# The opening of an encoder block's projection: unit differences of the second 512 tokens taken straight from PSUM, and the later unit parts stepped one product sooner per block

## The chip, the cores and the metric

The kernel runs on one core of a Trainium2 chip. The metric is the device time of one launch in microseconds; for each kernel the median of its runs is given. Engines are named as in the profile: PE is TensorE (matmuls and transposes), PEld its weight loads, DVE is VectorE, ACT is ScalarE, POOL is GpSimd, and SP is SyncE, on whose queue nearly all DMAs are issued in order.

## The reference, cut to what matters

The kernel computes one encoder block over S = 2048 tokens of width 1024, in float32: a norm, one wide projection cut in seven parts, differential attention with four heads, retention with eight heads in both directions, an output projection, and an MLP with squared relu. The change lies in the first two lines.

```python
h = rms_norm(x, norm1_g[l])
proj = h @ w_in[l]                       # 2048 x 1024 @ 1024 x 3584
dq, dk, dv, rq, rk, rv, rg = jnp.split(proj, offsets, axis=-1)   # seven parts of 512 columns
...                                      # attention, retention, norms, gate
x = x + mix @ w_out[l]
h = rms_norm(x, norm2_g[l])
u = jax.nn.relu(h @ w_mlp1[l])
x = x + (u * u) @ w_mlp2[l]
```

## The kernel before

**The projection.** It is done in two halves of 1024 tokens (g = 0 and 1) and, in each, in seven blocks of 512 columns, in the order rq, rk, rv, rg, q, k, v. A block is 1024 features x 512 columns of weights times 1024 features x 1024 tokens. It is computed by a Winograd scheme with seven products instead of eight: both operands are cut in quarters, the weights into a11, a12, a21, a22 and the tokens' side into b11, b21 (first 512 tokens, lower and upper 512 features) and b12, b22 (second 512 tokens). The products are, in this order, a11·b11, a12·b21, s2·t2, s1·t1, s3·t3, s4·b22 and a22·t4. The second factor is called the unit of the product (`UNITS` lists them in this order), with t1 = b12 − b11, t2 = b22 − t1, t3 = b22 − b12 and t4 = t2 − b21. s1 to s4 are sums and differences of weight quarters, made on POOL by tensor_tensor (L842, L849 and L275, tiles `s`).

**High and low parts.** Every float32 operand is split in a high part (rounded by a copy to the matmul's type) and a low part (value minus high part); a product is three matmuls, high·high (L36), high·low (L37) and low·high (L38). Weight quarters are split into `wh` (ScalarE, L44) and `wl` (VectorE, L50). A unit such as t2 has the tiles `t2h` and `t2l` of 128 x 4 x 512, four slices (kp = 0 to 3) of 128 features each. In the blocks rq and rk the result comes out by features (a matmul has 512 columns), from rv on by tokens (256 columns).

**The opening.** The units of g = 0 are made before and between the products of block rq by the class `FirstUnits`, and the engines' order there is the order of the code. For each slice kp, `turn` transposes the normalised x into PSUM tiles `htp` on TensorE (L198), `bring` copies one with the gain into SBUF tiles `usrc` on ScalarE (L208), `sub` makes differences of SBUF tiles (L216), on VectorE for t1 and t2, on POOL for t3 and t4, and `split` makes the two parts of a unit on engines given by name (L44 is ScalarE's high part, L46 POOL's, L50 a low part). `rest(kp)` strings these together for a slice; `parts()` runs `rest` of slices 1 to 4 between the first products.

**The second half's units.** They are made in the blocks rk, rv, rg and q of g = 0, 256 tokens in each. `second_load` brings 256 tokens (`x2`, L873, on SP), sums their squares on ScalarE (L773) and scales them on VectorE (L878). The generator `fill_parts` then does four steps: transposes (L178) brought with the gain (L181) and b11's split; t1, t3 (L146) and the splits of b21 and b22; t2, t4 and the splits of t1 and t3; the splits of t2 and t4. Each part goes to DRAM by a store on SP (L251). A step is taken in `between(unit)`, which `winograd_block` calls after each product:

```python
if UNITS.index(unit) > 2:
    next(fill, None)
```

so the four steps stand behind the products t1, t3, b22 and t4. The `x2` of the next block is loaded on SP behind the stores of the steps before. Weight tiles `raw` and `x2` share three buffers. All of the projection's products add up in eight PSUM banks, whose results VectorE adds to partial sums `c` (L316). For q and k a result by tokens is then normalised in groups of 64 (L713) and transposed back on TensorE (L750, into `pq`, split by L58 and L59).

Of the kernel before, what the change touches and what calls it, by code (L numbers as in the profile page):

```python
# [17 lines left out]
P = 128  # L18
# [58 lines left out]
H = G // 2  # L77
# [108 lines left out]
class FirstUnits:  # L186
# [14 lines left out]
    def bring(self, kp, kh, th):  # L201
        k = kh * 4 + kp
        if (kh, th) == (0, 1):
            t = self.pool2.tile([P, H], F32, tag="hi", name="usrc")
        else:
            t = self.pool.tile([P, H], F32, tag="c", name="usrc", bufs=BUFS["c"])
# [7 lines left out]
    def sub(self, kp, n, x0, x1, o, eng):  # L214
        b = self.b[kp]
        eng.tensor_tensor(out=o, in0=b[x0], in1=b[x1], op=ALU.subtract)  # L216
        b[n] = o

    def rest(self, kp):

        nc, b = self.nc, self.b
        if kp:
            self.split(kp - 1, "t3", "act")
        if kp < 3:
            self.bring(kp + 1, 0, 1)
            self.bring(kp + 1, 1, 1)
        if kp < 4:
            t2 = self.pool2.tile([P, H], F32, tag="hi", name="t2")
            self.sub(kp, "t1", "b12", "b11", b[kp]["b11"], nc.vector)
            self.sub(kp, "t2", "b22", "t1", t2[:], nc.vector)  # L230
            self.sub(kp, "t3", "b22", "b12", b[kp]["b12"], nc.gpsimd)
        if kp:
            self.split(kp - 1, "t4", "act")
        if kp < 4:
            self.split(kp, "t2", "act")
            self.sub(kp, "t4", "t2", "b21", b[kp]["b21"], nc.gpsimd)
            self.split(kp, "t1", *(("pool",), ("act",), ("pool",), ("act",))[kp])
            self.split(kp, "b22", "act", ("dve", "pool")[kp % 2])
# [329 lines left out]
def encoder(ctx: ExitStack, tc: tile.TileContext, a: dict, out: bass.AP, dbg=None):  # L568
# [129 lines left out]
    with ExitStack() as ph:  # L698
# [133 lines left out]
        for kp in range(4):  # L832
            fu.bring(kp, 1, 0)
            fu.split(kp, "b21", "pool")
        for kp in range(3):
            for kh in range(2):
                fu.turn(kp, kh, 1)
        fu.bring(0, 0, 1)
        fu.bring(0, 1, 1)

        s1, s2 = (wp.tile([P, 4, 256], F32, tag="s", name="s") for _ in range(2))
        nc.gpsimd.tensor_tensor(out=s1[:], in0=first[1][:, 0:4], in1=first[1][:, 4:8], op=ALU.add)  # L842
        fu.rest(0)
        ahead["a12"] = split_part(first[0][:, 4:8])

        def parts():
            fu.turn(3, 0, 1)
            fu.turn(3, 1, 1)
            nc.gpsimd.tensor_tensor(out=s2[:], in0=s1[:], in1=first[0][:, 0:4], op=ALU.subtract)  # L849
            fu.rest(1)  # L850
            yield
            ahead["s2"] = split_part(s2[:])
            for kp in range(2, 5):
                fu.rest(kp)
# [785 lines left out]
```

## Time and profile before

| | before |
|---|---|
| runs | 2843.67, 2831.81 and 2831.80 us, median 2831.81 |
| profiled execution | 2833.09 us |
| its span, first to last instruction | 2831.3 us |
| mean granted TensorE clock | 0.98 |
| opening to the last block in which x2 is brought | about the first 320 us of the span |

In a row of the timeline the first number is the start in microseconds from the span's start, the second the duration; then engine, line, operation, output <- inputs, partitions x elements, and in brackets the idle time before it and what ended it. Rows of the same kind in succession are put together, with their count behind an x. A row of waits reads: engine, what waited, what it waited for, and the total, the number and the longest of these waits. In a row of a window the engines' busy times stand in the order PE, PEld, DVE, ACT, POOL, with the granted clock of TensorE, the share of the DMA engines and GB/s at its end. A row of a line's operations has the smallest, the median and the greatest duration in nanoseconds.

### The profile page before, as it was taken

Reading aid. Unit: us, or ns where it says so; the run is one execution under the profiler, and the core shown is the slowest. Engines: PE = TensorE matmul, PEld = TensorE weight load, DVE = VectorE, ACT = ScalarE, POOL = GpSimd, SP = SyncE. Lnnn points to the kernel's source line nnn. Section 1 sums busy time; section 2 is a strip of 40 time slices with the busy share of each in tenths; the row PEclk is TensorE's granted clock in tenths of the full one; section 3 lists DMA queues with packets and bytes.
Section 4 is the critical chain, followed back from the end, with each engine's and each line's share of the span. In section 5 each row is a group of like instructions: output and inputs, shape, how many; then the busy total and the mean of one; then the engine's idle time right before and its main releaser. Section 6 shows DMA issues by size and latency. Waiting matters only on the chain.

```text
span 2831.3 us, 41049 instructions
## 1 busy us (share of the span) xinstructions
PE 2716.9 (96%) x15488; PEld 2332.9 (82%) x15488; DVE 1914.4 (68%) x2877; ACT 1297.6 (46%) x1842; POOL 1350.9 (48%) x778
## 2 busy tenths in 40 slices
PE   5998999998879999999898999999999999999999
PEld 4898889998768888888787788888888888888887
DVE  7878864587779999999898467665555534435442
ACT  5343432344457777777533255544445432222221
POOL 5326222613348787778544366765655104323320
PEclk8999999999899999999999999999999999999999
DMA  3555693249623131421368668767444858755471
GB/s 127 165 178 157 203 331 120 92 139 268 167 68 98 38 98 40 102 91 60 127 216 275 255 226 270 233 251 264 144 160 168 296 174 289 279 194 178 156 245 45
DMA packets 361029, 494.50 MB, mean 175 GB/s; under 512 B 23168, under 2 KB 257152, under 8 KB 352640
## 3 DMA queue, kind: packets, MB, share of 16 engines
q1 hardware_dynamic: 338608, 466.71, 50.4%
q10 hardware_dynamic: 21648, 20.98, 2.2%
q0 software_dynamic: 576, 4.19, 0.4%
q8 instruction: 122, 2.00, 0.3%
q14 instruction: 75, 0.61, 0.1%
HBM read 315.64 MB, written 176.16 MB: 174 GB/s over the span
## 4 chain that ended last, share of the span: by engine, by line
PE 75%; DVE 7%; DMA 4%; ACT 1%; issue 1%; POOL 1%; SPq 0%; ACTq 0%; DVEq 0%; POOLq 0%
PE ps L38 10%; PE ps L36 10%; PE ps L37 10%; PE p L38 7%; PE p L36 7%; PE p L37 7%; PE pa L1214 4%; PE sc L1020 4%; PE sc L1021 4%; PE po L36 2%; PE po L38 2%; PE po L37 2%; DVE kvs L493 1%; PE mm L38 1%; PE mm L37 1%
## 5 line engine op out<-in xcount | busy, mean ns | idle before, releaser
L37 PE MATMUL p<-wl,ah 128*128 128x512 f32 x896 | 348.6, 389 | 0.0
L36 PE MATMUL p<-wh,ah 128*128 128x512 f32 x896 | 348.5, 389 | 0.0
L275 POOL TENSOR_TENSOR s<-raw 128x1024 f32<-128x1024 f32 x58 | 147.6, 2545 | 402.5 <-DMA raw<-in_w_in 143.0
L50 DVE TENSOR_TENSOR wl<-s,wh 128x1024 fp32r<-128x1024 f32 x120 | 191.6, 1599 | 183.9 <-ACT wh L44 183.7
L316 DVE TENSOR_TENSOR c<-ps,c 128x512 f32<-128x512 f32 x360 | 238.4, 684 | 113.7 <-PE ps L38 111.6
L1053 POOL TENSOR_TENSOR p<-p 128x1024 f32<-128x1024 f32 x127 | 303.4, 2413 | 0.1
L44 ACT ACTIVATE ah<-ra 128x1024 fp32r<-128x1024 f32 x112 | 112.6, 1052 | 412.4 <-PE p L37 410.8
L1037 ACT ACTIVATE p<-p,nm 128x2048 f32<-128x2048 f32 x128 | 256.9, 2007 | 36.4 <-DVE nm L1025 35.1
L50 DVE TENSOR_TENSOR ah<-ra,ah 128x1024 fp32r<-128x1024 f32 x76 | 102.7, 1387 | 219.2 <-ACT ah L44 219.2
L1463 POOL TENSOR_TENSOR c<-c 128x512 f32<-128x512 f32 x128 | 196.4, 1560 | 111.3 <-ACT c L1466 101.8
L1524 POOL TENSOR_TENSOR t<-br 128x1024 f32<-128x1024 f32 x32 | 76.8, 2400 | 336.4 <-DMA br<-in_w_mlp 168.4
L38 PE MATMUL p<-wh,ah 128*128 128x512 f32 x608 | 236.6, 389 | 0.0
L44 ACT ACTIVATE wh<-s 128x1024 fp32r<-128x1024 f32 x120 | 126.4, 1056 | 200.0 <-PE ps L37 103.0
L1052 POOL TENSOR_SCALAR p<-p,ratio 128x1024 f32<-128x1024 f32 x127 | 141.9, 1131 | 143.3 <-DVE ratio L1047 111.2
L1020 PE MATMUL sc<-ka,qa 128*128 128x512 f32 x512 | 207.6, 406 | 2.6 <-DVE nm L1025 2.6
L1021 PE MATMUL sc<-ka,qb 128*128 128x512 f32 x512 | 202.9, 396 | 0.0
L37 PEld LDWEIGHTS p<-wl,ah 128*128 128x128 f32 x896 | 168.2, 188 | 34.9
L36 PEld LDWEIGHTS p<-wh,ah 128*128 128x128 f32 x896 | 168.2, 188 | 34.8
L55 ACT ACTIVATE aTh<-pa 128x512 fp32r<-128x512 f32 x256 | 151.2, 591 | 82.6 <-PE pa L1214 81.4
L1025 DVE CUSTOM_DVE_ANT_0 p<-sc,bias,nm 128x1024 f32<-128x1024 f32 (+1 forms) x136 | 167.7, 1233 | 22.6 <-PE sc L1021 20.8
L1214 PEld LDWEIGHTS pa<-ident,p 128*128 128x128 f32 x1024 | 121.1, 142 | 64.6 <-issue 30.7
L56 DVE TENSOR_TENSOR aTl<-pa,aTh 128x512 fp32r<-128x512 f32 x256 | 170.2, 686 | 4.4 <-DMA vh<-vhd 3.6
(377 smaller groups left out, 8164.9 us busy)
## 6 DMA issues: line engine op xcount, KB each, us to landing
br<-in_w_mlp SPq DMA_DIRECT2D x88, 512.0 KB, 5.3
raw<-in_w_mlp SPq DMA_DIRECT2D x32, 1024.0 KB, 5.9
raw<-in_w_in SPq DMA_DIRECT2D x28, 1024.0 KB, 5.9
xt<-in_x SPq DMA_DIRECT2D x20, 512.0 KB, 5.3
q<-rqd SPq DMA_DIRECT2D x16, 512.0 KB, 10.2
qa<-qhd SPq DMA_DIRECT2D x64, 128.0 KB, 2.9
qb<-qld SPq DMA_DIRECT2D x64, 128.0 KB, 3.0
ua11d<-c SPq DMA_DIRECT2D x32, 256.0 KB, 3.4
```

The costliest lines, as they stand in the source:

```text
L36: nc.tensor.matmul(out, ah, bh, start=first, stop=False)
L37: nc.tensor.matmul(out, ah, bl, start=False, stop=False)
L38: nc.tensor.matmul(out, al, bh, start=False, stop=last)
L44: nc.scalar.activation(hi, src, AF.Copy)
L50: e.tensor_tensor(out=lo, in0=src, in1=hi.bitcast(F32), op=ALU.subtract)
L316: nc.vector.tensor_tensor(out=o[:], in0=x0[:], in1=x1[:], op=op)
L1020: nc.tensor.matmul(sc[:, o : o + 512], qa[:, c, ql], r, start=True, stop=False)
L1021: nc.tensor.matmul(sc[:, o : o + 512], qb[:, c, ql], r, start=False, stop=True)
L1037: nc.scalar.activation(p[:], p[:], AF.Exp, bias=nm[:, n : n + 1], scale=-1.0, accum_out=l[:])
L1053: e.tensor_tensor(out=p0, in0=p0, in1=p1, op=ALU.add)
L1214: nc.tensor.transpose(pa[:, j], p0[:, kt * P : (kt + 1) * P], ident[:])
L1463: nc.gpsimd.tensor_tensor(out=u[n][:], in0=u[x0][:], in1=u[x1][:], op=op)
```

## The change

It has three parts. First, in the opening, the second 512 tokens' values no longer pass through SBUF for the differences: a new `times` computes gain · PSUM − x by one scalar_tensor_tensor on VectorE, for t1, t2, t3 and for the low part of b22 (L214 of the new kernel); `first` copies b12 and makes the high part of b22 straight from PSUM on ScalarE (L230, L232). The high parts of t1 to t4 are all ScalarE's (`high`, L225), their low parts VectorE's (`low`, L222); t4's subtraction stays on POOL (L243). Two of the four high parts of b21 go to ScalarE. Second, the order in the opening: a12's split moves ahead of the first slice's unit work, and the transposes of slices 2 and 3 move from ahead of and within b11's product to behind b21's. Third, the fill steps start behind t1 in block rk as before, behind t2 in rv, behind b21 in rg, and behind b11 in q.

```diff
--- before.py
+++ after.py
@@ -200,10 +200,7 @@
 
     def bring(self, kp, kh, th):
         k = kh * 4 + kp
-        if (kh, th) == (0, 1):
-            t = self.pool2.tile([P, H], F32, tag="hi", name="usrc")
-        else:
-            t = self.pool.tile([P, H], F32, tag="c", name="usrc", bufs=BUFS["c"])
+        t = self.pool.tile([P, H], F32, tag="c", name="usrc", bufs=BUFS["c"])
         ps = self.turned.pop((kp, kh, th))
         self.nc.scalar.activation(t[:], ps[:], AF.Copy, scale=self.gain[:, k : k + 1])
         self.b[kp][f"b{kh + 1}{th + 1}"] = t[:]
@@ -211,31 +208,52 @@
     def split(self, kp, n, hi, lo="dve"):
         split_sbuf(self.nc, *(t[:, kp] for t in self.tb[n]), self.b[kp][n], hi, lo)
 
-    def sub(self, kp, n, x0, x1, o, eng):
-        b = self.b[kp]
-        eng.tensor_tensor(out=o, in0=b[x0], in1=b[x1], op=ALU.subtract)
-        b[n] = o
+    def times(self, kp, kh, n, x, o):
+
+        k = kh * 4 + kp
+        self.nc.vector.scalar_tensor_tensor(
+            out=o, in0=self.turned[kp, kh, 1][:], scalar=self.gain[:, k : k + 1], in1=x, op0=ALU.mult, op1=ALU.subtract
+        )
+        if n is not None:
+            self.b[kp][n] = o
+
+    def low(self, kp, n):
+        th, tl = (t[:, kp] for t in self.tb[n])
+        self.nc.vector.tensor_tensor(out=tl, in0=self.b[kp][n], in1=th.bitcast(F32), op=ALU.subtract)
+
+    def high(self, kp, n):
+        self.nc.scalar.activation(self.tb[n][0][:, kp], self.b[kp][n], AF.Copy)
+
+    def first(self, kp):
+        nc, k = self.nc, 4 + kp
+        b12 = self.pool2.tile([P, H], F32, tag="hi", name="usrc")
+        nc.scalar.activation(b12[:], self.turned[kp, 0, 1][:], AF.Copy, scale=self.gain[:, kp : kp + 1])
+        self.b[kp]["b12"] = b12[:]
+        nc.scalar.activation(self.tb["b22"][0][:, kp], self.turned[kp, 1, 1][:], AF.Copy, scale=self.gain[:, k : k + 1])
 
     def rest(self, kp):
 
         nc, b = self.nc, self.b
+        if kp < 4:
+            b12 = b[kp]["b12"]
+            hi, lo = (t[:, kp] for t in self.tb["b22"])
+            self.times(kp, 0, "t1", b[kp]["b11"], b[kp]["b11"])
+            t2 = self.pool2.tile([P, H], F32, tag="hi", name="t2")
+            self.times(kp, 1, "t2", b[kp]["t1"], t2[:])
+            nc.gpsimd.tensor_tensor(out=b[kp]["b21"], in0=b[kp]["t2"], in1=b[kp]["b21"], op=ALU.subtract)
+            b[kp]["t4"] = b[kp]["b21"]
+            self.times(kp, 1, "t3", b12, b12)
+            self.times(kp, 1, None, hi.bitcast(F32), lo)
+            if (kp + 1, 0, 1) in self.turned:
+                self.first(kp + 1)
+            for n in ("t2", "t1", "t3"):
+                self.high(kp, n)
         if kp:
-            self.split(kp - 1, "t3", "act")
-        if kp < 3:
-            self.bring(kp + 1, 0, 1)
-            self.bring(kp + 1, 1, 1)
+            self.high(kp - 1, "t4")
+            self.low(kp - 1, "t4")
         if kp < 4:
-            t2 = self.pool2.tile([P, H], F32, tag="hi", name="t2")
-            self.sub(kp, "t1", "b12", "b11", b[kp]["b11"], nc.vector)
-            self.sub(kp, "t2", "b22", "t1", t2[:], nc.vector)
-            self.sub(kp, "t3", "b22", "b12", b[kp]["b12"], nc.gpsimd)
-        if kp:
-            self.split(kp - 1, "t4", "act")
-        if kp < 4:
-            self.split(kp, "t2", "act")
-            self.sub(kp, "t4", "t2", "b21", b[kp]["b21"], nc.gpsimd)
-            self.split(kp, "t1", *(("pool",), ("act",), ("pool",), ("act",))[kp])
-            self.split(kp, "b22", "act", ("dve", "pool")[kp % 2])
+            for n in ("t2", "t1", "t3"):
+                self.low(kp, n)
 
 
 def into_dram(nc, pool, tag, saved, j, tb=None):
@@ -831,25 +849,29 @@
         ahead = {"a11": split_part(first[0][:, 0:4])}
         for kp in range(4):
             fu.bring(kp, 1, 0)
-            fu.split(kp, "b21", "pool")
-        for kp in range(3):
+        for kp in range(4):
+            fu.split(kp, "b21", ("pool", "act")[kp % 2])
+        for kp in range(2):
             for kh in range(2):
                 fu.turn(kp, kh, 1)
-        fu.bring(0, 0, 1)
-        fu.bring(0, 1, 1)
 
         s1, s2 = (wp.tile([P, 4, 256], F32, tag="s", name="s") for _ in range(2))
         nc.gpsimd.tensor_tensor(out=s1[:], in0=first[1][:, 0:4], in1=first[1][:, 4:8], op=ALU.add)
+        fu.first(0)
+        ahead["a12"] = split_part(first[0][:, 4:8])
         fu.rest(0)
-        ahead["a12"] = split_part(first[0][:, 4:8])
 
         def parts():
-            fu.turn(3, 0, 1)
-            fu.turn(3, 1, 1)
             nc.gpsimd.tensor_tensor(out=s2[:], in0=s1[:], in1=first[0][:, 0:4], op=ALU.subtract)
             fu.rest(1)
             yield
+            yield
             ahead["s2"] = split_part(s2[:])
+            yield
+            for kp in range(2, 4):
+                for kh in range(2):
+                    fu.turn(kp, kh, 1)
+            fu.first(2)
             for kp in range(2, 5):
                 fu.rest(kp)
             opening.close()
@@ -925,7 +947,7 @@
                 def between(unit):
                     if g and what == "v":
                         lead_in(unit)
-                    if UNITS.index(unit) > 2:
+                    if UNITS.index(unit) > 3 - bi:
                         next(fill, None)
 
                 winograd_block(nc, wp, pp, raws, tb, what not in ("rq", "rk"), consumer(what, g), later, between,
```

On VectorE the opening's row from the first slice on was this before (`wl_392` is a12's low part, `t2_380` and `t2_425` are t2 of slices 0 and 1):

```order
28 L216 TENSOR_TENSOR usrc_287<-usrc_369,usrc_287 128x512
29 L216 TENSOR_TENSOR t2_380<-usrc_371,usrc_287 128x512
30 L50 TENSOR_TENSOR t2l_212<-t2_380,t2h_211 128x512
31 L50 TENSOR_TENSOR t1l_214<-usrc_287,t1h_213 128x512
32 L50 TENSOR_TENSOR b22l_218<-usrc_371,b22h_217 128x512
33 L50 TENSOR_TENSOR wl_392<-raw_203,wh_391 128x1024
34 L50 TENSOR_TENSOR t3l_216<-usrc_369,t3h_215 128x512
35 L216 TENSOR_TENSOR usrc_291<-usrc_376,usrc_291 128x512
36 L216 TENSOR_TENSOR t2_425<-usrc_378,usrc_291 128x512
```

and is this after:

```order
28 L50 TENSOR_TENSOR wl_366<-raw_203,wh_365 128x1024
29 L214 SCALAR_TENSOR_TENSOR usrc_287<-htp_339,g1_153,usrc_287 128x512
30 L214 SCALAR_TENSOR_TENSOR t2_370<-htp_344,g1_153,usrc_287 128x512
31 L214 SCALAR_TENSOR_TENSOR usrc_362<-htp_344,g1_153,usrc_362 128x512
32 L214 SCALAR_TENSOR_TENSOR b22l_218<-htp_344,g1_153,b22h_217 128x512
33 L222 TENSOR_TENSOR t2l_212<-t2_370,t2h_211 128x512
34 L222 TENSOR_TENSOR t1l_214<-usrc_287,t1h_213 128x512
35 L222 TENSOR_TENSOR t3l_216<-usrc_362,t3h_215 128x512
36 L214 SCALAR_TENSOR_TENSOR usrc_291<-htp_349,g1_153,usrc_291 128x512
37 L214 SCALAR_TENSOR_TENSOR t2_399<-htp_354,g1_153,usrc_291 128x512
```

The low part of a12 has moved from behind the first slice's lows to ahead of everything of that slice, and four operations of a slice read a PSUM tile `htp`. On POOL the row from b21 on was, before (`usrc <- usrc` is t3, `usrc <- t_380,usrc` is t4):

```order
L46 TENSOR_SCALAR b21h<-usrc 128x512 x4
L842 TENSOR_TENSOR s<-raw 128x1024
L216 TENSOR_TENSOR usrc<-usrc 128x512
L216 TENSOR_TENSOR usrc<-t_380,usrc 128x512
L46 TENSOR_SCALAR t1h<-usrc 128x512
L849 TENSOR_TENSOR s<-s,raw 128x1024
L275 TENSOR_TENSOR s<-raw,s 128x1024
L216 TENSOR_TENSOR usrc<-usrc 128x512
L216 TENSOR_TENSOR usrc<-t_425,usrc 128x512
```

and is after:

```order
L46 TENSOR_SCALAR b21h<-usrc 128x512 x2
L859 TENSOR_TENSOR s<-raw 128x1024
L243 TENSOR_TENSOR usrc<-t_370,usrc 128x512
L865 TENSOR_TENSOR s<-s,raw 128x1024
L293 TENSOR_TENSOR s<-raw,s 128x1024
L243 TENSOR_TENSOR usrc<-t_399,usrc 128x512
```

Two highs of b21, t3 and t1's highs have left POOL's row. On TensorE, in block rv, the 16 transposes of x2 stood between t1's and t3's products:

```order
L36 MATMUL ps<-wh,t1h 128x256
L37 MATMUL ps<-wl,t1h 128x256
L38 MATMUL ps<-wh,t1l 128x256
L178 MATMUL htp<-ident,x_1109 128x128 x16
L36 MATMUL ps<-wh,t3h 128x256
L37 MATMUL ps<-wl,t3h 128x256
L38 MATMUL ps<-wh,t3l 128x256
```

and stand between t2's and t1's now:

```order
L36 MATMUL ps<-wh,t2h 128x256
L37 MATMUL ps<-wl,t2h 128x256
L38 MATMUL ps<-wh,t2l 128x256
L178 MATMUL htp<-ident,x_1101 128x128 x16
L36 MATMUL ps<-wh,t1h 128x256
L37 MATMUL ps<-wl,t1h 128x256
L38 MATMUL ps<-wh,t1l 128x256
```

They have moved up by one product there; in the blocks rg and q they move up by two and by three.

## The prediction

> **What bounds the kernel now.** I read the page's totals first, then the waits of TensorE by stage, then the rows that end those waits.
>
> ```profile
> span 2831.3 us, 41049 instructions
> PE 2716.9 (96%) x15488; PEld 2332.9 (82%) x15488; DVE 1914.4 (68%) x2877; ACT 1297.6 (46%) x1842; POOL 1350.9 (48%) x778
> ```
>
> TensorE is busy for 96% of the span, so only its gaps, some 114 us, and slices at a lower clock can be won. The change touches the first 320 us, so I take TensorE's waits of 12 to 140 us (the opening), and of 111.8 to 330 us (the blocks in which the second 1024 tokens are filled).
>
> ```profile
> PE ps L38 <- DVE wl L50: 9.0, 3, 6.8
> PE ps L37 <- DVE t1l L50: 1.6, 1, 1.6
> PE ps L37 <- DVE t2l L50: 1.5, 1, 1.5
> PE ps L36 <- ACT t2h L44: 1.3, 1, 1.3
> ```
>
> ```profile
> PE pq L750 <- DVE c L713: 13.1, 2, 8.6
> PE ps L37 <- DVE wl L50: 5.7, 3, 2.4
> PE htp L178 <- DVE x L878: 2.3, 1, 2.3
> ```
>
> Nearly all of them end on VectorE. The opening ends for VectorE with the low part of s4's weights, for which the b22 product waits:
>
> ```profile
> 44.53 0.79 PE L38 MATMUL ps<-b21h,wl 128*128 128x512 f32 x1 [6.76 <-DVE wl L50]
> 80.32 0.49 PE L38 MATMUL ps<-b22h,wl 128*128 128x512 f32 x1
> 79.05 1.21 DVE L50 TENSOR_TENSOR wl<-s,wh 128x1024 fp32r<-128x1024 f32 x1
> ```
>
> Why VectorE is late there is seen in two pairs of rows, one pair with SBUF sources, one with PSUM sources:
>
> ```profile
> 37.70 2.33 POOL L849 TENSOR_TENSOR s<-s,raw 128x1024 f32<-128x1024 f32 x1
> 37.77 2.82 DVE L50 TENSOR_TENSOR t1l<-usrc,t1h 128x512 fp32r<-128x512 f32 x1 [1.76 <-POOL t1h L46]
> 43.26 1.21 DVE L50 TENSOR_TENSOR wl<-raw,wh 128x1024 fp32r<-128x1024 f32 x1
> 44.40 0.68 DVE L50 TENSOR_TENSOR t3l<-usrc,t3h 128x512 fp32r<-128x512 f32 x1
> 80.18 1.28 DVE L316 TENSOR_TENSOR c<-ps,c 128x512 f32<-128x512 f32 x2
> 80.40 2.40 POOL L275 TENSOR_TENSOR s<-raw,s 128x1024 f32<-128x1024 f32 x1 [4.82 <-DVE wl L50]
> ```
>
> A subtraction of two SBUF tiles takes 0.68 us alone (t3l) and 2.82 us when a POOL sum of 2.33 us runs (t1l ends 0.56 us after that sum). The two adds from PSUM, however, took 0.64 us each though POOL's sum covered most of them. I read it so: VectorE with two SBUF operands and POOL's tensor_tensor take turns; VectorE with one operand in PSUM does not wait.
>
> **The opening, part by part.** Removed: ScalarE's copy of b22 in each of the four slices (its high comes straight from PSUM), and on POOL four t3 subtractions, two b22 lows, two t1 highs. Added on VectorE: the four t3 and the two b22 lows that were POOL's; t1, t2, t3 and b22's low, 16 operations, now read PSUM. Added on ScalarE: two t1 highs and two b21 highs, less four copies, so it does no more than before, and at 46% of the span it has room. The price of the new form is not in the trace with this source; the nearest are these:
>
> ```profile
> 309.78 0.73 DVE L59 SCALAR_TENSOR_TENSOR lo<-pq,qg,hi 128x512 fp32r<-128x512 f32 x1
> 308.74 2.38 POOL L275 TENSOR_TENSOR s<-raw,s 128x1024 f32<-128x1024 f32 x1 [3.08 <-DVE wl L50]
> L316 DVE TENSOR_TENSOR c<-ps,c x12: 674/676/681, 76.7 to 86.8; 128x512 f32<-128x512 f32 x12
> 57.28 1.29 POOL L216 TENSOR_TENSOR usrc<-usrc 128x512 f32<-128x512 f32 x1 [1.23 <-DVE usrc L216]
> 27.43 5.51 DVE L50 TENSOR_TENSOR b21l<-usrc,b21h 128x512 fp32r<-128x512 f32 x4
> ```
>
> L59 is the same instruction (scalar times PSUM, minus SBUF): 0.73 us, inside a POOL sum of 308.74 to 311.12 and not held by it. Bounds: 0.68 us (a plain add from PSUM) and 2.8 us (if POOL holds it after all); I take L59's 0.73, or 0.67 from start to start, since successive rows overlap by some 0.07.
>
> With 0.67 per PSUM operation, 0.60 per free SBUF one, 1.15 per weight low, 2.35 per POOL sum and 1.25 per POOL subtraction, VectorE's new row runs as follows. The b21 lows end at 32.9 as before with a12's low now directly behind them: POOL does two highs instead of four, so it reaches its first sum about 1.2 us earlier, which pays for the 1.15. That low came at 43.26 to 44.47 before, and TensorE stood 6.76 us for it. Slice 0: four PSUM operations to 35.7, then t2, t1, t3 lows alternate with POOL's s2 and s4 sums (2 x 2.35) and its t4: 42.2. Slice 1: PSUM operations to 44.9, the late t4 low of slice 0 (ScalarE makes its high last) 46.4, three lows 48.2. Weight lows of s2 and s1, and slice 2's t1 from PSUM, one held by a POOL sum: 52.9. Slice 2's other three from PSUM, s3's low, four lows: 58.4. Slice 3's four: 61.1. Its predecessor's t4 low held by two sums for the next block's weights: 63.0. POOL's t4 64.2, remaining lows 66.6, four adds 69.0, s4's low 70.2. Before, that low ended at 80.26. The lead is **−10.1 us**. The lower bound of the gain is found by letting POOL hold the PSUM operations too: POOL's sums in that stretch would cost another 7.7 us, and 2.4 are left; the upper is 11 with 0.68 per operation less its overlap. TensorE can follow: its waits above (9.0 + 1.6 + 1.5 + 1.3 = 13.4) are more than the lead. The sixteen transposes of slices 2 and 3 move behind b21's product, but are the same in number; what was hidden on their account stays inside VectorE's row.
>
> [...]
>
> [...]
>
> **The fill steps.** Each of the next four blocks turns 256 tokens of the second half in four steps. All four blocks began them after the product t1; now the second, third and fourth begin one, two and three products sooner. No instruction is added. With its step move VectorE's and POOL's subtractions (L146), ScalarE's highs and the stores on SP; the stores pass the loads of the next block's weights, which are behind buffers in use, and POOL, 48% busy, takes its two subtractions a fill between weight sums. I put both at nothing so long as x2 is the last to come; it has its own term below. Old stalls first:
>
> ```profile
> 153.07 1.91 PE L178 MATMUL htp<-ident,x 128*128 128x128 f32 x16
> 154.83 0.36 PE L36 MATMUL ps<-wh,t3h 128*128 128x256 f32 x1
> 307.09 0.56 PE L36 MATMUL ps<-wh,t1h 128*128 128x256 f32 x1
> 147.31 0.28 PE L36 MATMUL ps<-wh,t1h 128*128 128x256 f32 x1
> 180.60:184.30 3.70, 3.70 (x19) 3.70 (x20) 3.39 (x5) 0.00 (x0) 0.16 (x1) 0.54 0.56 156
> 249.10:252.90 3.80, 3.35 (x17) 2.98 (x17) 3.66 (x6) 0.73 (x2) 0.00 (x0) 0.55 0.12 39
> 285.57 0.45 PE L750 MATMUL pq<-ident,c 128*128 128x128 f32 x1 [8.57 <-DVE c L713]
> ```
>
> A token-major product takes 5.75 us (147.31 to 153.07 holds one), sixteen transposes 1.76. From 153.07 to 307.09 there are 20 products, three sets of 16 transposes (5.3) and q's own transposes (L750), which I put at 3.5: 123.8 us of work in 154.0. So 30.2 us are lost, of them 21.1 as the waits above and the rest, 9.1, mostly as half clock (0.54 and 0.55 in two windows, behind waits of 2.3 us). The longest wait, 8.57, comes from VectorE's lateness in block q, where a fill step is done between 253 and 285.5:
>
> ```profile
> L50 DVE TENSOR_TENSOR hi<-x,hi 128x512 fp32r<-128x512 f32 x5 | 4.5, 893 | 0.0
> L181 DVE TENSOR_TENSOR x<-htp,g 128x512 f32<-128x512 f32 x4 | 2.6, 688 | 0.0
> L146 DVE TENSOR_TENSOR x<-x 128x512 f32<-128x512 f32 x2 | 1.8, 898 | 0.0
> ```
>
> These 8.9 us of VectorE's work move three products, 17 us, ahead, and the norm of q (L713) meets a free engine. Likewise the weight lows at a block's end (5.7) no longer meet the last fill step. I let 8.4 stand: what the two L750 waits leave beyond the 8.57 (13.1 − 8.6, say 5 with new ones), and two half-clock spells of 1.7. Gain **−21.8**, bounds 8.6 (that one wait alone) and 30.2.
>
> Now what comes in its place. TensorE asks for x2 sooner; x2 comes through SP's queue behind the last store of the fill before, is squared by ScalarE and scaled by VectorE.
>
> ```profile
> 137.67 0.59 SPq L873 DMA_DIRECT2D x<-in_x  x1
> 150.21 1.42 DVE L878 TENSOR_SCALAR x<-x,ss 128x1024 f32<-128x1024 f32 x2
> 183.73 0.95 SPq L873 DMA_DIRECT2D x<-in_x  x1
> 194.77 1.42 DVE L878 TENSOR_SCALAR x<-x,ss 128x1024 f32<-128x1024 f32 x2
> 249.16 0.64 PE L178 MATMUL htp<-ident,x 128*128 128x128 f32 x2 [2.32 <-DVE x L878]
> ```
>
> In rv the transposes now stand where t1 began, 147.31, and the first half of x2 is scaled at 150.9 (half of the 1.42 row): a wait of 3.6. Both shift with the opening's lead, since rk's steps keep their places. In rg and q the round from one set of transposes to the next has 36.3 us (six products and 1.76). It needs 1.76, three products (17.25), about 6 for the last split and its store (the last step no longer sits at the block's end), 1.5 on the queue, 11.1 from x2's issue to its scaling (183.73 to 194.77), and 0.7: 38.3. So 2.0 each. Half clock costs 1.7 behind the first wait (the 180.60 window: 3.7 x 0.46). Behind waits of 2.0, a little shorter than those for which a row shows it, it costs between 0 and 1.7 each; I take the middle, 1.7 for both. Price **+11.0**, from 3.6 (the two rounds fit) to 28.3 (the first rival).
>
> [...]
>
> **Sum.** −10.1 − 21.8 + 11.0 = −20.9 against the profiled execution's 2833.1: 2812.2. That execution lies 1.3 above the median of the runs, so 2811.
>
> **The rivals.** First, x2 takes all back: if the rounds stay as long as before (153.07 to 195.5 is 42.4, 199.25 to 249.16 is 49.9), the waits are 3.6 + 6.1 + 13.6 and 5 of half clock, 28.3 in all; −3.6, or 2828. For it: SP's queue is in order and x2 stands behind the stores. Against: those two rounds contained the very stalls that go. Second, PSUM operations are held by POOL too: lead 2.4, 2819. Against it stand L59 and the 80.18 row. Third, slower: the x2 wait feeds itself. Each round as long as the longest, 49.9, because the scaling (L878) stands in VectorE's row behind weight lows that themselves wait for POOL's sums of weights, whose load is behind x2 on SP: 3 x 13.6 + 5 = 45.8, net +13.9, 2846. It decides once the three waits with their clock pass 31.9. Only one round of three showed this length. A fourth, that the DVE row is no bound for TensorE in the opening, is refuted by the waits quoted.
>
> **How the numbers follow.** Forecast 0.67, first rival 0.18, second 0.08, third 0.07. A change below 0.5% (14.2 us, 2817.7 to 2846) can hardly be told from none. The forecast's own range is 2799 (all 30.2 gained, waits near 6) to 2820, with about a tenth of its chance above 2817.7; rivals one and two lie within 0.5%. So faster 0.60, same 0.33, slower 0.07. The range is 2799 to 2829: it takes in rivals one and two and leaves out the third and the ends.
>
> **What would show it.** The b21 product without the 6.76 wait; SCALAR_TENSOR_TENSOR from `htp` at 0.73 to 0.75 while POOL runs; the b22 product at s4's low ten us sooner; no long L750 wait in q; new waits of the L178 transposes on x in rv near 3.6 and in rg and q near 2. Waits there of 6 and more would show the first rival or the third; PSUM rows of 2 us and more the second.

## The result and the profile after

The changed kernel takes 2816.5 us (median of five runs, 2814.8 to 2820.8) against 2834.9 for the kernel before in the same comparison (2831.8 to 2843.7): the ratio is 0.994, interval 0.9929 to 0.9951, or 18.4 us less. The forecast was 2811, and faster. The profiled execution of the changed kernel took 2819.9, 3.4 above its median, with a span of 2818.2.

The page's totals and TensorE's waits, first in the opening (12 to 140 us), then in the blocks in which the second half is filled (100 to 330 us), after the change (lines of the new kernel: L198 and L178 are the same transposes, L900 was L878, L768 was L750, L731 was L713). The waits for the normalised x ahead of the first products stand in both kernels, 17.7 us before and 16.7 after, and are left out:

```profile
span 2818.2 us, 41052 instructions
PE 2716.7 (96%) x15488; PEld 2332.3 (83%) x15488; DVE 1906.4 (68%) x2883; ACT 1298.4 (46%) x1844; POOL 1329.9 (47%) x768
```

```profile
PE htp L198 <- DVE usrc L214: 2.8, 1, 2.8
PE ps L36 <- DVE usrc L214: 2.3, 1, 2.3
PE ps L36 <- ACT wh L44: 1.6, 1, 1.6
PE ps L37 <- DVE t1l L222: 1.5, 1, 1.5
PE htp L198 <- DVE b22l L214: 1.1, 1, 1.1
PE ps L36 <- DVE b22l L214: 0.6, 1, 0.6
```

```profile
PE htp L178 <- DVE x L900: 11.0, 3, 6.9
PE pq L768 <- DVE rst L71: 1.2, 1, 1.2
PE pq L768 <- DVE c L731: 0.9, 1, 0.9
PE ps L36 <- DVE lo L59: 0.4, 1, 0.4
```

The 6.8 us for a12's low are gone, but new waits of 9.9 us stand in the opening, four of the six on operations that read PSUM (L214). In the fill, 21.1 us of waits have become 13.5, of which 11.0 are for x2. Three marks divide the span, the first scores of the attention (L1020, now L1042), the last of that line, and the first matmul of the MLP (L36 into `p`). Of before, then of the changed kernel:

```profile
L1020 PE MATMUL sc<-ka,qa x512: 388/396/795, 794.9 to 1355.2; 128*128 128x512 f32 x171
...
L36 PE MATMUL p<-wh,ah x896: 388/389/390, 2217.9 to 2826.5; 128*128 128x512 f32 x180
```

```profile
L1042 PE MATMUL sc<-ka,qa x512: 389/396/792, 778.4 to 1338.8; 128*128 128x512 f32 x171
...
L36 PE MATMUL p<-wh,ah x896: 389/389/389, 2204.8 to 2813.4; 128*128 128x512 f32 x180
```

With the first transposes of x2 in rk (111.8 before, 107.0 after) the 13.1 us of the two profiled spans split so: 4.8 in the opening, 11.7 from there to the attention, nothing in the attention, 3.3 given back between its end and the MLP (862.7 us before, 866.0 in this execution). This last loss looks like this execution's own and not the change's: in the eight other kernels of the table whose POOL rows stand there in the same order (before, opening only, SBUF source, sums behind, a12 first, POOL relieved, gain on VectorE, same late order) the stretch takes 862.2 to 863.4 us. The experiments are read by the same marks:

| run | opening, lead | to the attention | attention's end to MLP | median against before in the same comparison |
|---|---|---|---|---|
| before | 0 | 683.1 | 862.7 | |
| changed | 4.8 | 671.4 | 866.0 | −18.4 |
| opening only | 4.9 | 682.9 | 863.2 | −6.5 |
| steps only | −1.0 | 670.1 | 872.2 | −3.4 |
| SBUF source | 5.4 | 671.7 | 863.4 | −19.6 |
| sums behind | 7.9 | 676.3 | 862.2 | −19.7 |
| q later | 3.8 | 670.6 | 862.5 | −15.2 |
| a12 first | 0.3 | 683.9 | 863.0 | +0.5 |
| POOL relieved | 4.4 | 680.0 | 863.3 | −5.0 |
| one gate multiplication (one run) | 8.3 | 663.2 | 861.9 | −29.3 |
| relief and steps | 4.6 | 670.4 | 872.8 | −7.0 |
| gain on VectorE | 7.6 | 668.1 | 862.7 | −22.6 |
| gate on VectorE | 7.7 | 667.0 | 869.1 | −17.4 |
| same late order | 3.4 | 671.2 | 862.7 | −13.4 |

The stages are of one profiled execution each; the last column is of the timed runs. The changed kernel, opening only and q later have the same opening, and its lead is 4.8, 4.9 and 3.8. In q later VectorE's row there is only 0.1 us later, but behind the wait of 2.3 us at t3's product TensorE's granted clock was 0.67 from 64.1 to 71.6 us, where the changed kernel's was 0.81. So leads that differ by 1 us are not told apart.

### The profile page after: what moved, and what is told of

It is laid out like the page before. It is cut to its first block, busy times and chain, and to the rows that moved or that the text cites. A ratio compares the mean times of both kernels' runs of the same rounds, so it can differ in the third digit from the quotient of the medians.

```text
span 2818.2 us, 41052 instructions
## 1 busy us (share of the span) xinstructions
PE 2716.7 (96%) x15488; PEld 2332.3 (83%) x15488; DVE 1906.4 (68%) x2883; ACT 1298.4 (46%) x1844; POOL 1329.9 (47%) x768
## 4 chain that ended last, share of the span: by engine, by line
PE 79%; DVE 7%; DMA 2%; issue 1%; ACT 1%; POOL 1%; SPq 0%; ACTq 0%; DVEq 0%; POOLq 0%
PE ps L38 11%; PE ps L36 11%; PE ps L37 11%; PE p L38 7%; PE p L36 7%; PE p L37 7%; PE pa L1236 4%; PE sc L1042 4%; PE sc L1043 4%; PE po L36 2%; PE po L38 2%; PE po L37 2%; DVE kvs L511 1%; PE mm L38 1%; PE mm L37 1%
## 5 line engine op out<-in xcount | busy, mean ns | idle before, releaser
L36 PE MATMUL p<-wh,ah 128*128 128x512 f32 x896 | 348.4, 389 | 0.0
L1042 PE MATMUL sc<-ka,qa 128*128 128x512 f32 x512 | 207.5, 405 | 3.2 <-ACT yt L575 2.7
L36 PEld LDWEIGHTS p<-wh,ah 128*128 128x128 f32 x896 | 168.2, 188 | 34.9
L1047 DVE CUSTOM_DVE_ANT_0 p<-sc,bias,nm 128x1024 f32<-128x1024 f32 (+1 forms) x136 | 167.7, 1233 | 22.6 <-PE sc L1043 21.0
## 6 DMA issues: line engine op xcount, KB each, us to landing
q<-rqd SPq DMA_DIRECT2D x16, 512.0 KB, 10.1
```

The lines of the kernel that those rows point to most:

```text
L36: nc.tensor.matmul(out, ah, bh, start=first, stop=False)
L1042: nc.tensor.matmul(sc[:, o : o + 512], qa[:, c, ql], r, start=True, stop=False)
```

## The experiments

My theory after the result was that both parts work as forecast, and that the opening is 5 us short because two POOL sums for the next block's weights run in the middle of it. The rival was that reading PSUM keeps the banks and makes TensorE the bound.

**The two parts alone.** First the changed kernel with the old fill steps:

```diff
-                    if UNITS.index(unit) > 3 - bi:
+                    if UNITS.index(unit) > 2:
```

> The changed opening with the old fill steps (behind t1 in all four blocks). If the two parts are worth what the trace of the changed kernel shows, block rk's first transposes of x2 come at 107.0 us of the span as there (111.8 before), a lead of 4.8, the stalls from 153 to 307 us stay, and the time is 4.8 us under before, about 2830. The rival: the lead lets the middle run differently, x2 and the weights come relatively sooner and part of the old stalls goes too; then 8 to 13 us under before.

2828.3 against 2834.7, ratio 0.9978 (0.9970 to 0.9987). By stage it is the theory: a lead of 4.9, 682.9 us to the attention as before. Then the reverse, the kernel before with the new steps:

```diff
-                    if UNITS.index(unit) > 2:
+                    if UNITS.index(unit) > 3 - bi:
```

> The kernel before with only the earlier fill steps. The two traces give 195.3 us from rk's transposes to the start of k's t1 product before and 185.5 after: if that stretch's gain is the steps' own, the time is 9.8 us under before, about 2825. The rival: the gain needs the opening's lead (x2 of rv comes later against the products), then waits for x2 of about 11 take the gain back and the time is within 3 us of before.

2831.3 against 2834.7, ratio 0.9984 (0.9975 to 0.9992): only 3.4 less, which looks like the rival, but isn't. From rk's transposes to the attention it takes 13.0 us less than before, 10.8 of them up to k's t1 product; x2's waits did not take it back. It lost 9.5 far behind, between the attention and the MLP. TensorE's waits there, of before (1355.2 to 2217.9) and of this run (1344.3 to 2216.5):

```profile
PE mt L1186 <- POOL mx L1177: 2.8, 4, 0.9
...
PE mt L1186 <- POOL mx L1176: 2.0, 2, 1.3
```

```profile
PE mt L1186 <- POOL mx L1176: 11.9, 6, 3.5
...
PE mt L1186 <- POOL mx L1177: 1.2, 3, 0.6
```

`mt` are the transposes of the attention's and retention's mixed output ahead of the output projection. No line of that code differs. The rows do: the built program of this run has POOL's multiplications of `mx` (L1176, L1177) behind a low part of the next units, where they stood ahead of it (`+` is this run's place):

```order
 L1379 TENSOR_SCALAR early<-xt_15393,rs_15777 128x1024
-L1176 TENSOR_TENSOR mx<-mx,dog 128x512
-L1177 TENSOR_TENSOR mx<-mx,gates 128x512
 L50 TENSOR_TENSOR hl_15845<-quads,hl_15844 128x512
+L1176 TENSOR_TENSOR mx<-mx,dog 128x512
+L1177 TENSOR_TENSOR mx<-mx,gates 128x512
```

So the order of a stage that the scheduler arranges changed with an edit more than 1000 us ahead of it. In the changed kernel it did not. The last experiment tests this.

**Where the operands come from.** In the changed kernel b12 and b22 are copied to SBUF by ScalarE, and VectorE's differences read the copies (ScalarE's added copy of b22 is not shown here):

```diff
-        self.nc.vector.scalar_tensor_tensor(
-            out=o, in0=self.turned[kp, kh, 1][:], scalar=self.gain[:, k : k + 1], in1=x, op0=ALU.mult, op1=ALU.subtract
-        )
+        self.nc.vector.tensor_tensor(out=o, in0=self.b[kp][f"c{kh + 1}2"], in1=x, op=ALU.subtract)
```

> The changed kernel, but b12 and b22 are copied to SBUF by ScalarE first, and t1, t2, t3 and b22's low on VectorE are plain subtractions of SBUF tiles in the same order. If reading PSUM is what lets VectorE run beside POOL, the operations that now run during POOL's four t4 subtractions (1.3 us each) must take turns with them: 5.2 us more in VectorE's row, less 16 x 0.06 for the shorter form, so 4 us over the changed kernel, with nearly all of its lead in the opening gone. The rival: the PSUM tiles now come free by ScalarE, the transposes behind b21 no longer wait (2.8 and 1.2 us in the changed kernel), and the form costs less, so the time is the same or up to 3 us less.

2815.1 against 2834.7, ratio 0.9928 (0.9916 to 0.9941): not told apart from the changed kernel's 0.994. Both readings were right in their part, and they cancel. b22's low of slice 0, first in the changed kernel, then from SBUF beside POOL's t4:

```profile
35.34 0.74 DVE L214 SCALAR_TENSOR_TENSOR b22l<-htp,g,b22h 128x512 fp32r<-128x512 f32 x1
```

```profile
34.58 1.62 POOL L243 TENSOR_TENSOR usrc<-t,usrc 128x512 f32<-128x512 f32 x1 [4.97 <-DVE t L213]
...
34.95 1.79 DVE L213 TENSOR_TENSOR b22l<-usrc,b22h 128x512 fp32r<-128x512 f32 x1
```

From SBUF it is held by POOL, about 1.0 us in each of four slices, and VectorE's last low ends at 71.5 instead of 70.0. But in the changed kernel t3's product on TensorE waits for VectorE to read a bank (L214 makes t1 of slice 3 there, which t3's product doesn't need, and in the run from SBUF this wait is gone, so I put it down to the bank), and then VectorE waits 1.6 us for that product's result:

```profile
64.02 0.77 PE L36 MATMUL ps<-t3h,wh 128*128 128x512 f32 x1 [2.33 <-DVE usrc L214]
...
71.64 0.69 DVE L334 TENSOR_TENSOR c<-ps,c 128x512 f32<-128x512 f32 x1 [1.63 <-PE ps L38]
```

The result is the same to within what is measured. (The transposes' waits for banks, 2.8 and 1.2 us, cost nothing of their own: t2's product starts at 48.0, and at 48.4 in the run from SBUF, where it waits for s2's high part instead.)

**The next block's sums.** In the changed kernel these two sums are put behind slice 3's t4 on POOL; no row of VectorE or TensorE moves:

```diff
-        nc.gpsimd.tensor_tensor(out=t[:], in0=wa[x0], in1=wa[x1], op=op)
+        with behind(n):   # for s1, s2 of block rk: tc.issue_after(fu.last.ins)
+            nc.gpsimd.tensor_tensor(out=t[:], in0=wa[x0], in1=wa[x1], op=op)
```

> The changed kernel with POOL's two sums for the next block's weights (2.6 and 2.7 us at 57.3 and 60.0 us) put behind the t4 subtraction of slice 3; nothing else moves on VectorE or TensorE. If these sums are why the opening's lead was 5 us short, slice 2's t1 and t3 lows take 0.7 us instead of 2.9 each, VectorE's row is 4.4 us earlier from there, TensorE's wait of 2.3 at t3's product goes, and the time is 3 to 4.5 us under the changed kernel. The rival: TensorE's own row, with its transposes that waited for PSUM banks, is the bound by then (VectorE stood 1.6 us waiting for it at 71.6), and the time is less than 1 us under, or over if the sums then come late for block rk.

2815.0 against 2834.7, ratio 0.9926 (0.9913 to 0.9940). The lead at rk is 7.9 instead of 4.8 (7.6 and 7.7 in two later runs with the sums behind), so the sums do cost the opening some 3 us, as the theory had it. VectorE and POOL of the changed kernel, then with the sums behind:

```profile
57.32 2.56 POOL L293 TENSOR_TENSOR s<-raw 128x1024 f32<-128x1024 f32 x1 [1.96 <-DMA raw<-in_w_in]
57.57 2.86 DVE L222 TENSOR_TENSOR t1l<-usrc,t1h 128x512 fp32r<-128x512 f32 x1
59.96 2.70 POOL L293 TENSOR_TENSOR s<-s,raw 128x1024 f32<-128x1024 f32 x1
60.36 2.85 DVE L222 TENSOR_TENSOR t3l<-usrc,t3h 128x512 fp32r<-128x512 f32 x1
```

```profile
57.28 0.68 DVE L222 TENSOR_TENSOR t1l<-usrc,t1h 128x512 fp32r<-128x512 f32 x1
57.88 0.68 DVE L222 TENSOR_TENSOR t3l<-usrc,t3h 128x512 fp32r<-128x512 f32 x1
```

The time, however, did not fall by 3 to 4.5. k's t1 product still starts 3.0 us earlier than in the changed kernel (289.5 and 292.5), though q's x2 waits 9.1 instead of 6.9 us. Then 4.8 us are lost on the way to the attention. TensorE's wait for ScalarE in the retention there, in the changed kernel and with the sums behind:

```profile
PE rt L573 <- ACT yT L565: 4.6, 1, 4.6
```

```profile
PE rt L574 <- ACT yT L566: 10.3, 2, 6.6
```

That is 5.7 us in a stage whose rows are the same in both; why ScalarE came later there I have not traced.

**Order alone and load alone.** The kernel before with a12's split ahead of the first slice:

```diff
+        ahead["a12"] = split_part(first[0][:, 4:8])
         fu.rest(0)
-        ahead["a12"] = split_part(first[0][:, 4:8])
```

> The kernel before with nothing changed but a12's split put ahead of the first slice's unit work. If the order is what gives the opening's lead, b21's wait of 6.8 us for that low part goes and rk's first transposes come 4 to 5 us earlier, like the changed opening alone. The rival: VectorE and POOL have the same work to do in turns, the unit lows come later by what the weight low takes, and the lead is at most 1.5 us (the low takes 1.2).

2834.3 against 2833.8, ratio 1.0003 (0.9994 to 1.0011), a lead of 0.3. The rival was right: the wait moved one product on and grew from 6.8 to 9.7.

```profile
48.91 0.79 PE L36 MATMUL ps<-t2h,wh 128*128 128x512 f32 x1 [9.73 <-ACT wh L44]
```

Then the kernel before in its order and from SBUF, with POOL's work taken away as in the change, at three places of the code:

```diff
-            fu.split(kp, "b21", "pool")
+            fu.split(kp, "b21", ("pool", "act")[kp % 2])
-            self.sub(kp, "t3", "b22", "b12", b[kp]["b12"], nc.gpsimd)
+            self.sub(kp, "t3", "b22", "b12", b[kp]["b12"], nc.vector)
-            self.split(kp, "t1", *(("pool",), ("act",), ("pool",), ("act",))[kp])
-            self.split(kp, "b22", "act", ("dve", "pool")[kp % 2])
+            self.split(kp, "t1", "act")
+            self.split(kp, "b22", "act")
```

> The kernel before in its old order and from SBUF copies, but POOL relieved as in the change: t3 and all b22 lows on VectorE, all t1 highs and two b21 highs on ScalarE. POOL loses some 4 x 1.25 + 2 x 1.25 + 4 x 0.6 = 9.9 us, VectorE gains 6 x 0.6 = 3.6; if taking turns is the bound, the sum of both rows is 6 us shorter and the lead at rk's transposes is 4 us or more. The rival: only the order brings the lead, and here it is under 1.5 us, or negative, since VectorE's own row is longer.

2828.8 against 2833.8, ratio 0.9985 (0.9976 to 0.9994), a lead of 4.4. To within what leads can tell, that is the whole of the opening's 4.8: POOL's relief is enough for it, without the PSUM source and without the new order. VectorE's own row did gain by the other two, since its last low part ends at 76.7 us before, at 73.2 with relief alone, at 71.5 in the run from SBUF (relief and order) and at 70.0 in the changed kernel. TensorE did not follow, and little of that reached block rk.

**q's x2.** Its transposes waited 6.9 us where I had put 2. One try gives it a product more:

```diff
-                    if UNITS.index(unit) > 3 - bi:
+                    if UNITS.index(unit) >= (0, 3, 2, 1, 1, 0, 0)[bi]:
```

> The changed kernel with block q's steps one product later (behind b21, as in rg; rk and rv as changed). If x2 of q is ready at 228.7 us whatever TensorE asks, its transposes stand then after the b21 product (end at 227.4) and wait 1.3 instead of 6.9 and 0.6, and the half clock behind them goes: k's t1 product 5 to 6 us earlier, and the time 4 to 6 us less. The rival: the fill's work on VectorE moves against q's own norms, whose waits (8.6 before, 1.2 and 0.9 in the changed kernel) come back by as much, and the time is within 2 us of the changed kernel.

2818.6 against 2833.8, ratio 0.9947 (0.9934 to 0.9959): no better than the changed kernel. x2's wait fell to 1.7 and 1.1, but q's norms wait again, as the rival had it:

```profile
261.60 0.45 PE L768 MATMUL pq<-ident,c 128*128 128x128 f32 x1 [5.80 <-DVE c L731]
```

The other try leaves out the gate's second multiplication on POOL (the output lacks the retention's norm gain):

```diff
-                    nc.gpsimd.tensor_tensor(
-                        out=t3, in0=t3, in1=gng[:, c0 : c0 + 256].unsqueeze(1).to_broadcast([P, 2, 256]), op=ALU.mult
-                    )
```

> The changed kernel without the second POOL multiplication of the gate (by the retention's group norm gain) in block rg, of both halves, so the output lacks that factor. If POOL's multiplications hold VectorE's small operations and the scaling of q's x2 (from 221.4 to 230.2 us, where 6 to 7 us pass for 2.4 us of work), the wait of q's transposes falls from 6.9 to 4 us or less. The rival: x2 of q is late by its load and by ScalarE's queue (its squares end at 219.4), and the wait stays between 6 and 7.5.

One run of 2804.5. q's x2 waited 2.4 us and then 1.1. In the changed kernel, two rows of x2's chain beside the gate's multiplications:

```profile
224.47 2.31 POOL L750 TENSOR_TENSOR c<-c,gng 128x512 f32<-128x512 f32 x1
...
225.59 1.22 DVE L73 SCALAR_TENSOR_TENSOR ss<-rst,ss 128x2 f32<-128x2 f32 x1
226.84 3.39 DVE L900 TENSOR_SCALAR x<-x,ss 128x1024 f32<-128x1024 f32 x2
```

Here an operation on 128 x 2 elements takes 1.22 us, which took 0.16 at 145.23 us, where POOL was idle, and the scaling 3.39 instead of 1.42. So the rows show the theory's mechanism, POOL's gate holding x2's chain, but it is not the whole of the shorter wait. From its first small operation to the end of the scaling the chain took 10.6 us in the changed kernel (219.65 to 230.23) and 8.6 without the second multiplication. The longest hold in it, 2.26 us for another operation on 128 x 2 elements, lay beside a weight sum of POOL (222.18 to 224.51), and it stayed. Of the 4.4 us by which the wait fell, some 2.0 are the chain's. The rest came because x2's load was issued 6.7 us sooner (203.2 instead of 209.9) while TensorE asked only 4.2 sooner; why it was, I have not traced. By accident this run showed more. In its opening the first sum for the next block started at 57.68 instead of 57.32, 0.02 after slice 2's t1 low had started:

```profile
57.68 2.91 POOL L293 TENSOR_TENSOR s<-raw 128x1024 f32<-128x1024 f32 x1 [2.23 <-DMA raw<-in_w_in]
...
57.66 0.68 DVE L222 TENSOR_TENSOR t1l<-usrc,t1h 128x512 fp32r<-128x512 f32 x1
58.27 2.87 DVE L222 TENSOR_TENSOR t3l<-usrc,t3h 128x512 fp32r<-128x512 f32 x1
```

One turn fell the other way, and rk's transposes came at 103.5 instead of 107.0. Of these 3.5 us the turn gave 2.1, the time by which VectorE's last low ends earlier (67.9 instead of 70.0). For the rest TensorE's granted clock was 1.00 instead of 0.81 from 64.1 to 71.6 us, behind a wait of 2.0 instead of 2.3.

**A version meant to do more.** The changed kernel with the sums behind, and with that second multiplication on VectorE instead:

```diff
-                    nc.gpsimd.tensor_tensor(
+                    nc.vector.tensor_tensor(
                         out=t3, in0=t3, in1=gng[:, c0 : c0 + 256].unsqueeze(1).to_broadcast([P, 2, 256]), op=ALU.mult
```

> The changed kernel with the next block's two sums behind slice 3 (as in the run of that edit alone) and the gate's second multiplication in rg moved from POOL to VectorE. On POOL it takes 1.3 to 1.7 us in which VectorE's SBUF work waits, on VectorE 0.7: eight of them in the first half, 5 us less of turns, most of it between 196 and 235 us. Then the wait of q's transposes (9.1 with the sums behind) falls to 5 or less and the time is 4 to 5 us under that run, near 2810. The rival: VectorE's row gets longer just ahead of x2's scaling, the wait stays above 7, and the time is within 1.5 us of that run.

2811.7 against 2834.4, ratio 0.9926 (0.9912 to 0.9939), 3.3 below the run with the sums behind by medians, whose ratio is the same; so the two are not told apart. The reason I gave is refuted: q's x2 waits 10.4 us, not 5, since the multiplications now stand in VectorE's own row ahead of the scaling. The gain to the attention (668.1 instead of 676.3) came elsewhere: 2.0 us up to k's t1 product, with q's norms never waiting, and 7.2 in that retention wait for `yT`, 3.1 instead of 10.3; 1.0 of these 9.2 was lost again elsewhere. With the first multiplication moved too:

```diff
-                    nc.gpsimd.tensor_tensor(out=t[:], in0=t[:], in1=sg[:], op=ALU.mult)
+                    nc.vector.tensor_tensor(out=t[:], in0=t[:], in1=sg[:], op=ALU.mult)
```

> As the run before it, and the gate's first multiplication on VectorE too, so POOL has none of the gate. If turns alone count, another 5 us of them go, q's transposes wait 2 to 3 us, and the time is 6 to 9 us under the run with the sums behind, near 2808. The rival: the first multiplication needs ScalarE's sigmoid, VectorE stands in order behind it and with it the partial sums and x2's scaling, and the time is 2 us or more above the run with only the second multiplication moved.

2817.0 against 2834.4, ratio 0.9941 (0.9929 to 0.9954). From rk's transposes to the attention it is the fastest of the runs that leave nothing out, by 1.1 us, with q's x2 waiting 7.8. Then it lost 6.4 between attention and MLP (869.1 against 862.7), where its rows stand in another order again; whether that order made the loss is not tested. So its median speaks for the rival, but not for the rival's reason.

**The whole without source and order.** The kernel before with POOL relieved and the new steps:

> The kernel before, in its old order and from SBUF copies, with POOL relieved as in the run of that edit alone, and with the earlier fill steps. If reading PSUM and the new order are worth nothing, this has the whole of the change: 15 to 19 us under before, though the two parts alone were 5.0 and 3.4 under. The rival: the two parts simply add, or the new order is what keeps the steps' gain, and it is 7 to 11 us under before.

2827.4 against 2834.4, ratio 0.9978 (0.9969 to 0.9987): 7.0 less, and by the time alone the rival. By stage it is at the attention's end at 1337.5, ahead of the changed kernel's 1338.8, and then takes 872.8 us to the MLP. Its late rows stand as in the run of the steps alone. Leaving t1's two highs on POOL happens to restore them:

```diff
-            self.split(kp, "t1", "act")
+            self.split(kp, "t1", *(("pool",), ("act",), ("pool",), ("act",))[kp])
```

> The kernel before, in its opening's old order and from SBUF copies, with the earlier fill steps and POOL relieved as before but for t1's two highs, which stay on POOL. The point of that exception: the rows of every engine in the output projection stand then as in the kernel before, while in the two runs with the steps on the old opening they stood otherwise there (the mixed tiles' transposes waited 10 to 12 us for POOL instead of 5). If that other late order is what cost those runs some 9.5 us, this one has nearly the whole of the change, 15 to 18 us under before, with the output projection's stretch from 1338 on at 863 us as before, not 872. The rival: the loss belongs to the steps on the old opening or to something that the new order and the PSUM source mend, and it is 6 to 9 us under before as those were.

2819.1 against 2832.6, ratio 0.9957 (0.9943 to 0.9971). The marks and the waits from 1339.8 to 2202.5:

```profile
L1020 PE MATMUL sc<-ka,qa x512: 389/396/796, 779.6 to 1339.8; 128*128 128x512 f32 x171
...
L36 PE MATMUL p<-wh,ah x896: 389/389/390, 2202.5 to 2811.1; 128*128 128x512 f32 x180
```

```profile
PE mt L1186 <- POOL mx L1177: 2.2, 4, 0.8
```

The stretch is 862.7 us again and the long waits on POOL are gone, with one unit split between the two runs; the loss was that of the late order. Not every other order costs: in the run with q later POOL's rows stand in a third order there, with the multiplications still ahead of the low parts, and the stretch takes 862.5 us. The median gain of 13.4 is a little under the 15 expected. The changed kernel's is 18.4, but the intervals of the two ratios (0.9943 to 0.9971 and 0.9929 to 0.9951) overlap, so it is not shown whether the PSUM source and the new order add some us to the whole or nothing. The opening's lead is 3.4 with those two highs back on POOL.

## Why the prediction was right, and where its terms were off

The direction was right, and the time lies 5.5 us above the forecast, inside its range. By its steps:

- **The opening, −10.1 forecast, −4.8 measured.** This is the term that failed. VectorE's walk was right for two slices: slice 1's lows were forecast to end at 48.2, and they end at 48.6. It failed at slice 2, where I let POOL's sums for the next block hold one late low (1.9 us) and they held two lows for 2.86 and 2.85. VectorE's last low ends 3.4 us behind the walk (70.0 instead of 66.6), and VectorE then stood another 1.6 for the result of TensorE's t3 product. The run with the sums behind gives 3.1 of the 5.3 back. The second error was the sentence that TensorE can follow: its old waits went, but 9.9 us of new ones came, of which t3's product (2.3) and part of t1's (0.6) stood, as I read the rows, only for a bank that VectorE had yet to read. I counted transposes and no banks. Nor did the opening's sum have any half clock, as the fill's sum had: from 64.1 to 71.6 us, behind t3's wait, the granted clock was 0.81, which I estimate at 1.4 us (0.19 of 7.5).
- **The PSUM source.** Its price was right: L214 takes 0.741 us (median of eight, with L59's 0.73 as the forecast), and no row of 16 was held, so the rival that POOL holds them is out. The form is 0.06 above the plain subtraction from SBUF (0.68 in the run from SBUF), but the plain add from PSUM is not: in the kernel before it took 0.676 (L316, median of twelve) and t1's subtraction of SBUF tiles 0.678 (L216, median of four). What was wrong is its worth: 1.5 us on VectorE's row, and by the time of the run from SBUF nothing that could be told apart.
- **Old stalls −21.8 and new waits +11.0, together −10.8.** This sum ends at k's t1 product, and up to there 9.8 were won (195.3 us from rk's transposes before, 185.5 after), with the steps alone 10.8. By the prediction's own count, 129.5 us of work from 142.7 to 292.5, 20.3 us are lost where 19.4 were forecast. From there to the attention another 1.9 were won, with the steps alone 2.2, where I had put nothing. The idle waits of the old list fell by 18.6 (21.1 to 2.5), and 11.0 of x2's came. That these waits equal the price of 11.0 is chance, since the price held 7.6 of waits and 3.4 of half clock. In rv the wait was 3.57 as forecast (3.6), and the sixteen transposes behind it took 3.67 us instead of 1.91, close to the 1.7 of half clock. Other sizes were off: rg none where I had 2, q 6.9 and 0.6 where I had 2. In q the mis-sized step is the 11.1 us from x2's issue to its scaling: it took 10.9 in rg (172.83 to 183.75) and 17.0 in q (209.87 to 226.84), where POOL's gate and a weight sum held operations of x2's chain. The third rival also had the scaling late in VectorE's row, but behind weight lows that wait for their sums; that is another mechanism, and the delay came in one block of three, so it did not decide.
- **After the attention.** I put nothing there. In the changed kernel's profiled execution 3.3 us were lost, with rows in the same order as before; the two waits on POOL are 5.6 us against 4.8, the rest I can't name. Other kernels with the same order there do not lose it. Two experiments, however, lost 9.5 and 10.1 by another order, so a forecast of 0 was not safe.
- **The total.** It lies near the forecast partly by luck. The terms as measured in the two profiled executions give −4.8 − 11.7 + 3.3, some 13 us, where −20.9 was forecast and the medians show −18.4: the profiled execution of before lies 1.8 us below its median, that of the changed kernel 3.4 above. The opening's missing 5.3 us were made up in part by gains on the way to the attention that the sum did not have.

## What to carry to other kernels

Taking work off the engine that shares turns with the bottleneck was worth more here than where the bottleneck's operands lie: POOL's relief alone gave a lead of 4.4 us and the whole new opening 4.8, while reading PSUM shortened VectorE's row by 1.5 us and paid for it in waits of TensorE that I put down to banks (2.3 and 0.6). Before a source is moved from SBUF to PSUM, count who waits for the bank. And where a scheduler arranges the rows, compare them in stages that the edit does not touch: an edit worth 12.0 us at the attention's first scores showed 3.4 at the end because a stage 1000 us later had been reordered.

## What the runs showed of the hardware that was not expected

- In the changed kernel VectorE's operations on 128 x 2 elements took 1.22 us beside a gate multiplication of POOL and 2.26 beside one of its weight sums, against 0.16 with POOL idle. So small operations were held too, and a tensor_scalar of one SBUF operand with per-partition scalars (L900): 3.39 us for two that took 1.42 with POOL idle.
- A fraction of a microsecond decided a turn: in the run with one gate multiplication a sum that a DMA released 0.36 us later let one low pass (0.68 us instead of 2.86), and VectorE's row was 2.1 us shorter.
- A short wait of TensorE had no fixed price in clock. In three runs with the same opening (changed, q later, one gate multiplication) the waits at t3's product were 2.33, 2.35 and 2.00 us, and the granted clock from 64.1 to 71.6 us was 0.81, 0.67 and 1.00. The product's matmuls behind its first, 0.39 us each in the last of these runs, took 0.63 up to 66.7 us in the first and up to 68.1 in the second.
